# Hybrid decoder layer on one core: FFN weight loads behind the memory output's, GpSimd sums begun behind the second merged tile, last splits and tail reordered

## The chip, the cores and the metric

The kernel runs on 1 core of one Trainium2 chip. The metric is device time in microseconds (us). Engines are named as in the profile: PE is TensorE (matmuls; PEld its weight loads), DVE is VectorE, ACT is ScalarE, POOL is GpSimd, SP issues DMAs. A name with a q (SPq, POOLq) is the engine's queue that issues DMAs. Every engine works through its own list of instructions in order; semaphores tie the lists together.

## What is computed

One layer of a decoder for 512 tokens of width 1024, in float32, cut to what matters:

```python
h = rms_norm(x, g_mix)
q, k, v, u, gb, gc, ga, gB = split(h @ w_in)            # 3 x 512, 3 x 512, 2 x 1024 columns
o_a = stick_breaking_attention(q, k, v)                 # 8 heads of 64, causal
y_b = gb * causal_conv3(gc * u)                         # 512 channels
merged = sigmoid(ga) * (o_a @ w_a) + sigmoid(gB) * (y_b @ w_b)
x = x + merged @ w_mix_out
x = x + cross_attention(rms_norm(x), rms_norm(mem)) @ w_mem_o    # 4 heads of 256, 256 memory tokens
gate, up = split(rms_norm(x) @ w_ffn_in)                # 2 x 2816 columns
x = x + (silu(gate) * up) @ w_ffn_out
return rms_norm(x, g_final)
```

## The kernel before, in words

Matmuls run in a reduced float32 format, so each factor is split into a high part (a cast on ACT) and a low part (the difference, on DVE), and each product is three matmuls: high x high, high x low, low x high (`mm3`, L148 to L151). A weight tile therefore goes SP load (`wr`), ACT cast (`wh`), DVE subtraction (`wl`), PE; `load_w` (L133 to L146) does this for all weights up to the memory output, and the pool behind `wr`, `wh` and `wl` has 4 buffers each.

The stages, in order of time: value projection; projections of q, k, conv and gates, interleaved with the attention; the merge (L479 to L497: eight tiles m, each two gate projections, the two branch products `br`, two sigmoids, products with the gates on DVE at L493, their sum at L494, and a split `mh`, `ml`); key projection of the memory (`km`, L500 to L512) and value projection (`vm`, L513 to L525); the mix output and residual; the memory's queries and attention (L587 to L651); the memory output and residual (L653); the FFN (L657 to L893); the output product (`run`, L898); and the tail with the last norm (L1038 to L1071).

FFN input and output products are computed with seven products of half tiles in place of eight. For the output product this needs sums of blocks of `w_ffn_out`. GpSimd makes them ahead (L450 to L461): for each of 11 pieces j it loads 1 MB into a tile `pre`, adds four times in place (L458) and stores the tile to a DRAM tile `sums` (L460). The pool `prepool` has two such tiles. It opens when the attention's pool `lpool` closes (L450) and when it closes `fpool` takes its memory (L462).

`ffn_load` (L664) loads one FFN tile m on SP in three loads: `ws` (L670), `wg` (L672), `a` (L674; `a22` in the code); a DMA of GpSimd (L675) adds onto `ws`. Tiles of m = 0 and 1 are loaded for the first eight products. Most of them take `wr` buffers, and some, the `a` of m = 0, the `ws` of m = 1 and the `wg` of m = 2, take tiles of `fpool`.

Outside the two stretches under `manual_schedule` (the first tiles, and all from L848 on) a scheduler sets the order of each engine's list; `after` (L101) adds an ordering without a semaphore. From L848 on PE, ACT and DVE follow the order in which the code is written. There, `uses` (L760) lists the products (m, i) of FFN tile m; `reads` and `second` take a product's bank into SBUF, `evict` applies the norm, Silu and the product with the other half, in three parts. `first_parts` (L831) is a list of preparations for the output product: `out_pair` loads and splits two blocks of weights, `act_first` and `act_second` split activations. The first of them are popped among the last FFN products (L883), the others beside `run`.

In the output product, `run(i, j)` is product i of seven on piece j (six matmuls). After products 0 to 3, the loop from L1002 runs products 4, 6 and 5, with `act_third`, `out_pair` and `out_one` as their preparations, and adds two transposed tiles of the residual per step (`turned`, `begin`). The tail adds product 5, forms the squares on ACT, the factor of the last norm from them (`rstd`: a sum on DVE, Ln and Exp on ACT, a correction step on DVE), scales the eight output tiles and stores them.

Of the kernel before, what the change touches and what calls it, by code (L numbers as in the profile page):

```python
# [33 lines left out]
FIRST = 4  # L34

# [4 lines left out]
def hybrid_layer(ctx: ExitStack, tc: tile.TileContext, xT_d, memT_d, cols_d, wv_d, win_d,  # L40
# [58 lines left out]
    exps, casts, lead, lows = [], [], [], []  # L99
# [33 lines left out]
    def load_w(src, cols=P):  # L133
# [3 lines left out]
        i = nc.sync.dma_start(raw, src)  # L137
        if count[1] < FIRST:
            count[1] += 1
            chained(i)  # L140
# [312 lines left out]
    with tc.tile_pool(name="prepool", bufs=2) as prepool:  # L453
        for j in range(NJ):
            t = prepool.tile([P, 4, 512], F32, tag="pre", name=nm("pre"))
            nc.gpsimd.dma_start(t, wfo_d[j])
# [5 lines left out]
    fpool = ctx.enter_context(tc.tile_pool(name="fpool", bufs=2))  # L462

    mg = []
# [15 lines left out]
    for m in range(KD):  # L480
# [14 lines left out]
        merged.append(split(sig[0], "m"))  # L495
        if m % 2 == 1:
            mem_split(m // 2)  # L497

# [165 lines left out]
    def ffn_load(m):  # L664
# [5 lines left out]
        nc.sync.dma_start(s13, a[:, 2:3, :].broadcast_to([P, 2, 512]))  # L670
        wg = wg[0].tile([P, 2, 512], F32, tag=wg[1], name=nm("wg"))
        nc.sync.dma_start(wg, a[:, 0:2, :])  # L672
        a22 = fpool.tile([P, 512], F32, tag="w2", name=nm("a22"), bufs=4)
        nc.sync.dma_start(a22, a[:, 3, :])  # L674
# [173 lines left out]
    with tc.manual_schedule(engines={mybir.EngineType.PE, mybir.EngineType.Activation,  # L848
# [6 lines left out]
        for n, (m, i) in enumerate(uses):  # L855
# [6 lines left out]
            elif i == 5 and m == NF - 1:  # L862
                reads(m, i)
                second(m)
            else:
                if i == 1 and m > 0:
                    second(m - 1)
                reads(m, i)
# [14 lines left out]
            if n >= len(uses) - 6 and n % 2 == len(uses) % 2:  # L883
                first_parts.pop(0)()
            if (m, i) == (NF - 2, 6):
                evict(m, 0)
                evict(m, 1)
            if (m, i) == (NF - 1, 5):
                evict(NF - 2, 2)
        evict(NF - 1, 0)  # L890
# [79 lines left out]

        def turned(t, h):
# [6 lines left out]
        def begin(t, h, x):  # L978
            if t < 2 and h == 0:
# [3 lines left out]
                nc.gpsimd.tensor_tensor(out=l1[t], in0=l1[t], in1=gain[0], op=ALU.mult)  # L983
# [17 lines left out]
        lag = 1  # L1001
        for j in range(NJ):  # L1002
            if j + 2 < NJ and j > 0:
                act_third(j + 1)
            if j < NJ - 2:
                run(4, j)
                if j == 0:
                    uv = [plus("uv", res[2][s2], u[s2]) for s2 in range(2)]
                    res[5] = [ztile("p5") for _ in range(2)]
                settle()  # L1010
                if j > 0:
                    out_pair(j + 1, sums[j + 1][:, 2:4, :], 4, 6)
                run(6, j)
                out_one(j + 1)
                if j >= lag:
# [119 lines left out]
```

## Time and profile before

| What | Value |
|---|---|
| Median of 3 runs | 896.61 us (893.87 to 896.71) |
| The profiled execution's own time | 894.85 us |
| Its span on the core | 893.1 us |
| TensorE busy | 853.7 us (96%) |
| VectorE busy | 647.2 us (72%) |
| ScalarE busy | 459.2 us (51%) |
| GpSimd busy | 145.4 us (16%) |
| Granted TensorE clock, mean | 0.98 |
| DMA, mean | 156 GB/s |

The profile is of one execution; its span is the time from its first to its last instruction on the core, and 1.75 us of its own time lie around that. Start times in the rows are us from the span's start. A row of waits gives the waiting engine and line, what ended the wait, the total in us, how often, and the longest. A row of the timeline gives start, duration, engine, line and operation, output and inputs, and in brackets how long the engine sat idle before it and what ended that. A busy TensorE isn't one at full speed: its clock is shown apart, as granted by the throttle.

### The profile page before, as it was taken

Reading aid. Unit: us, or ns where it says so; the run is one execution under the profiler, and the core shown is the slowest. Engines: PE = TensorE matmul, PEld = TensorE weight load, DVE = VectorE, ACT = ScalarE, POOL = GpSimd, SP = SyncE. Lnnn points to the kernel's source line nnn. Section 1 sums busy time; section 2 is a strip of 40 time slices with the busy share of each in tenths; the row PEclk is TensorE's granted clock in tenths of the full one; section 3 lists DMA queues with packets and bytes.
Section 4 is the critical chain, followed back from the end, with each engine's and each line's share of the span. In section 5 each row is a group of like instructions: output and inputs, shape, how many; then the busy total and the mean of one; then the engine's idle time right before and its main releaser. Section 6 shows DMA issues by size and latency. Waiting matters only on the chain.

```text
span 893.1 us, 12825 instructions
## 1 busy us (share of the span) xinstructions
PE 853.7 (96%) x4840; PEld 743.2 (83%) x4840; DVE 647.2 (72%) x1080; ACT 459.2 (51%) x842; POOL 145.4 (16%) x179
## 2 busy tenths in 40 slices
PE   9999999998999964999999999999999999999994
PEld 7888888886888854888888889999999999888883
DVE  7778879988655634645554678977888788799765
ACT  7466666664233223444344466555554555566544
POOL 0022211216566550000000010111111110000011
PEclk9999999999999996999999999999999999999998
DMA  7322222227787648542212153777766773366532
GB/s 284 122 103 83 83 83 64 78 72 283 276 300 283 236 189 282 182 149 95 95 48 71 48 129 83 189 198 178 181 179 178 191 189 94 116 216 209 189 130 95
DMA packets 48574, 139.54 MB, mean 156 GB/s; under 512 B 4608, under 2 KB 6656, under 8 KB 45696
## 3 DMA queue, kind: packets, MB, share of 16 engines
q1 hardware_dynamic: 38576, 103.04, 34.4%
q0 software_dynamic: 9216, 34.61, 14.7%
q10 hardware_dynamic: 720, 1.07, 0.3%
q8 instruction: 38, 0.62, 0.3%
q14 instruction: 24, 0.20, 0.1%
HBM read 125.07 MB, written 13.63 MB: 155 GB/s over the span
## 4 chain that ended last, share of the span: by engine, by line
PE 80%; POOL 8%; DMA 7%; DVE 2%; ACT 1%; issue 1%; SPq 0%; ACTq 0%; DVEq 0%; POOLq 0%
PE z L706 14%; PE p L903 11%; POOL pre L458 8%; PE y L706 7%; DMA pre<-in_w_ffn_out_dram 6%; PE pr L150 5%; PE pr L149 5%; PE pr L151 5%; PE v L706 4%; PE r L150 3%; PE r L149 3%; PE r L151 3%; PE v L255 3%; PE mq L149 2%; PE mq L150 2%; PE mq L151 2%
## 5 line engine op out<-in xcount | busy, mean ns | idle before, releaser
L144 ACT CAST wh<-wr 128x1024 fp32r<-128x1024 f32 x84 | 88.0, 1051 | 188.7 <-issue 77.8
L145 DVE TENSOR_TENSOR wl<-wr,wh 128x1024 fp32r<-128x1024 f32 x84 | 108.6, 1295 | 59.9 <-ACT wh L144 59.8
L149 PE MATMUL pr<-xgh,wh 128*128 128x512 f32 x288 | 113.3, 393 | 2.3 <-DVE g L493 2.3
L150 PE MATMUL pr<-xgl,wh 128*128 128x512 f32 x288 | 113.2, 393 | 0.0
L151 PE MATMUL pr<-xgh,wl 128*128 128x512 f32 x288 | 112.7, 391 | 0.0
L675 POOL DMA_DIRECT2D ws<-in_w_ffn_in_dram x22 | 26.5, 1207 | 358.9 <-DVE c L535 170.4
L458 POOL TENSOR_TENSOR pre<-pre 128x512 f32<-128x512 f32 x44 | 67.4, 1536 | 28.4 <-DMA pre<-in_w_ffn_out_dram 26.1
L706 PE MATMUL z<-xdh,wf 128*128 128x256 f32 x352 | 70.5, 283 | 0.2 <-ACT sb L727 0.2
L149 PEld LDWEIGHTS pr<-xgh,wh 128*128 128x128 f32 x288 | 54.4, 189 | 13.9 <-DVE g L493 2.7
L151 PEld LDWEIGHTS pr<-xgh,wl 128*128 128x128 f32 x288 | 54.5, 189 | 11.5
L150 PEld LDWEIGHTS pr<-xgl,wh 128*128 128x128 f32 x288 | 54.5, 189 | 10.9
L706 PEld LDWEIGHTS z<-xdh,wf 128*128 128x128 f32 x352 | 58.0, 192 | 0.5 <-ACT sb L727 0.4
L727 ACT COPY sa<-z 128x256 f32<-128x256 f32 x44 | 16.4, 372 | 79.3 <-PE z L706 78.4
L706 PE MATMUL z<-xdl,wf 128*128 128x256 f32 x176 | 49.8, 283 | 0.0
L696 DVE TENSOR_TENSOR wf<-s,wf 128x512 fp32r<-128x512 f32 x44 | 30.3, 691 | 25.8 <-ACT wf L695 25.7
L813 DVE TENSOR_TENSOR wl<-wr,wh 128x1024 fp32r<-128x1024 f32 x33 | 40.7, 1232 | 9.8 <-ACT wh L812 9.8
L812 ACT CAST wh<-wr 128x1024 fp32r<-128x1024 f32 x33 | 34.6, 1049 | 11.3 <-PE p L903 5.5
L149 PE MATMUL km<-mgh,wh 128*128 128x256 f32 x64 | 19.2, 304 | 19.3 <-DVE km L506 19.3
L706 PE MATMUL y<-xoh,wf 128*128 128x256 f32 x176 | 35.6, 285 | 1.8 <-DVE sb L737 1.8
L706 PE MATMUL z<-xch,wf 128*128 128x256 f32 x176 | 35.4, 284 | 0.1
L706 PE MATMUL y<-xch,wf 128*128 128x256 f32 x176 | 35.4, 283 | 0.0
L706 PE MATMUL v<-xoh,wf 128*128 128x256 f32 x176 | 35.4, 283 | 0.0
(315 smaller groups left out, 2437.0 us busy)
## 6 DMA issues: line engine op xcount, KB each, us to landing
wr<-in_w_in_dram SPq DMA_DIRECT2D x36, 512.0 KB, 3.5
pre<-in_w_ffn_out_dram POOLq DMA_DIRECT2D x11, 1024.0 KB, 8.4
sums<-pre POOLq DMA_DIRECT2D x11, 1024.0 KB, 4.9
ws<-in_w_ffn_in_dram SPq DMA_DIRECT2D x22, 512.0 KB, 3.7
wg<-in_w_ffn_in_dram SPq DMA_DIRECT2D x22, 512.0 KB, 4.1
ws<-in_w_ffn_in_dram POOLq DMA_DIRECT2D x22, 512.0 KB, 5.9
wr<-sums SPq DMA_DIRECT2D x22, 512.0 KB, 4.6
wr<-in_w_ffn_out_dram SPq DMA_DIRECT2D x16, 512.0 KB, 3.7
```

The source lines that it names most:

```text
L144: after(nc.scalar.copy(h2, raw), lead[-1:])
L145: lows.append(nc.vector.tensor_tensor(out=l2, in0=raw, in1=f(h2), op=ALU.subtract))
L149: nc.tensor.matmul(ps, a[0], b[0], start=start, stop=False, **kw)
L150: nc.tensor.matmul(ps, a[0], b[1], start=False, stop=False, **kw)
L151: nc.tensor.matmul(ps, a[1], b[0], start=False, stop=stop, **kw)
L255: nc.tensor.matmul(vps[t], xg[k][a][:, sl], wv[k][b], start=k == 0 and (a, b) == (0, 0), stop=k == KD - 1 and a == 1)
L458: nc.gpsimd.tensor_tensor(out=t[:, a, :], in0=t[:, a, :], in1=t[:, b, :], op=ALU.add)
L696: nc.vector.tensor_tensor(out=w[:, 1, :], in0=raw, in1=f(w[:, 0, :]), op=ALU.subtract)
L706: nc.tensor.matmul(ps[:, :HS], a, b, start=i < 3 and k == 0 and j == 0, stop=k == KP - 1 and j == 2, skip_group_check=True)
L812: nc.scalar.copy(hi, raw)
L813: nc.vector.tensor_tensor(out=lo, in0=raw, in1=f(hi), op=ALU.subtract)
L903: nc.tensor.matmul(res[i][s2], a[:, ts], b, start=j == 0 and n == 0, stop=j == NJ - 1 and n == 2)
```

## The change

Four things are changed.

- `load_w` keeps its load instructions in a list. The first FFN loads (m < 2) are ordered behind the sixth from last of them, `loads[-6]`, which is the third of the eight loads of the memory output.
- The sums are made by a function that is called in the merge, behind the split of the second merged tile (`SUMS_AT = 1`). For the first two pieces a copy of one column of that tile into `pre` on GpSimd makes the load wait for it. `prepool` opens as before, and closes, with `fpool` opening, behind the merge.
- Among the last FFN products, `second` of the last tile is called one product earlier and ahead of the eviction, and the first parts are popped after products -6, -3 and -1 from the end, not -6, -4 and -2.
- In the output product the third split and the pair of weights are prepared for j + 2 in every step, not for j + 1. In the tail, the factor of token tiles 2 and 3 is begun before the last product, its correction step comes later (`rstd_end`), the second product for tiles 2 and 3 gets its gain on GpSimd (`gained`), scalings are divided anew between ACT and DVE (`how`), and all stores but one go through SP.

```diff
+SUMS_AT = 1
...
         i = nc.sync.dma_start(raw, src)
+        loads.append(i)
...
+    def weight_sums(prepool):
         for j in range(NJ):
             t = prepool.tile([P, 4, 512], F32, tag="pre", name=nm("pre"))
+            if j < 2:
+                nc.gpsimd.tensor_copy(t[:, 0, 0:1], f(merged[SUMS_AT][0])[:, 0:1])
             nc.gpsimd.dma_start(t, wfo_d[j])
...
         merged.append(split(sig[0], "m"))
+        if m == SUMS_AT:
+            weight_sums(prepool)
...
-        nc.sync.dma_start(s13, a[:, 2:3, :].broadcast_to([P, 2, 512]))
+        i = nc.sync.dma_start(s13, a[:, 2:3, :].broadcast_to([P, 2, 512]))
+        if m < 2:
+            after(i, [loads[-6]])
...
-            elif i == 5 and m == NF - 1:
-                reads(m, i)
-                second(m)
...
-            if n >= len(uses) - 6 and n % 2 == len(uses) % 2:
-                first_parts.pop(0)()
             if (m, i) == (NF - 2, 6):
+                second(NF - 1)
                 evict(m, 0)
                 evict(m, 1)
             if (m, i) == (NF - 1, 5):
                 evict(NF - 2, 2)
+            if n - len(uses) in (-6, -3, -1):
+                first_parts.pop(0)()
...
+        for j in range(NJ - 2):
+            run(4, j)
...
+            settle()
+            act_third(j + 2)
+            run(6, j)
+            out_pair(j + 2, sums[j + 2][:, 2:4, :], 4, 6)
+            if j > 0:
+                run(5, j - 1)
+            out_one(j + 1)
...
+        for s2 in range(2):
+            onto(ys[2 + s2, 0], res[6][s2], 2 + s2, ys[2 + s2, 0])
+            square(2 + s2, 0)
+            gained(2 + s2, 0)
...
+        rstd(hi)
+        end(0)
+        rstd_end(hi)
+        store(2, 1, "act")
+        store(2, 0, "dve")
+        rstd(t0)
+        end(1)
+        store(3, 1, "act")
+        rstd_end(t0)
+        store(0, 1, "both")
+        store(0, 0, "act")
+        rstd(t1)
+        store(3, 0, "dve")
+        rstd_end(t1)
+        store(1, 1, "both")
+        store(1, 0, "act")
```

The same treatment as `s13` gets goes for `wg` and `a22`. How the lists of instructions change is shown at three places.

SP in the key projection, before: `wr` from `w_mem_k` are key weights, `a`, `ws` and `wg` FFN loads.

```order
L137 DMA wr_3246<-in_w_mem_k_dram 128x1024
L674 DMA a_4971<-in_w_ffn_in_dram 128x512
L670 DMA ws_4976<-in_w_ffn_in_dram 128x2x512
L137 DMA wr_3281<-in_w_mem_k_dram 128x1024
L672 DMA wg_5090<-in_w_ffn_in_dram 128x1024
L137 DMA wr_3318<-in_w_mem_k_dram 128x1024
L137 DMA wr_3353<-in_w_mem_k_dram 128x1024
```

SP in the memory output, of the changed kernel: `wr` from `w_mem_o` are that stage's weights.

```order
L138 DMA wr_4585<-in_w_mem_o_dram 128x1024
L138 DMA wr_4620<-in_w_mem_o_dram 128x1024
L138 DMA wr_4678<-in_w_mem_o_dram 128x1024
L690 DMA a_4973<-in_w_ffn_in_dram 128x512
L682 DMA ws_4978<-in_w_ffn_in_dram 128x2x512
L686 DMA wg_5092<-in_w_ffn_in_dram 128x1024
L138 DMA wr_4715<-in_w_mem_o_dram 128x1024
```

The three FFN loads left the key projection, where now the eight key loads follow each other, and stand behind the third load of the memory output.

ACT at the end of the FFN, before: `wh` are weight casts of `out_pair`, `f01h` and `f26h` activation casts, `fg` the Silu of FFN tiles 20 and then 21.

```order
L812 CAST wh_7885<-wr_7883 128x1024
L163 CAST f01h_7889<-a_5551 128x512
L746 ACTIVATE fg_7669<-fg_7669 128x512
L812 CAST wh_7923<-wr_7921 128x1024
L163 CAST f26h_7929<-a_5285 128x512
L796 CAST f_7933<-n_7927 128x256
L746 ACTIVATE fg_7799<-fg_7799 128x512
L108 ACT_TABLE_LOAD
L812 CAST wh_7972<-wr_7970 128x1024
```

The same place on ACT in the changed kernel:

```order
L764 ACTIVATE fg_7671<-fg_7671 128x512
L830 CAST wh_7903<-wr_7901 128x1024
L165 CAST f01h_7907<-a_5553 128x512
L830 CAST wh_7943<-wr_7941 128x1024
L165 CAST f26h_7949<-a_5287 128x512
L814 CAST f_7953<-n_7947 128x256
L764 ACTIVATE fg_7801<-fg_7801 128x512
L109 ACT_TABLE_LOAD
L830 CAST wh_7974<-wr_7972 128x1024
```

The first Silu moved ahead of the casts of the second piece (`wh_7903`, `f01h_7907`); the last Silu, the table load and the cast of that piece's second pair stay where they were.

DVE in the tail, before: `u_8504` is an eviction of product 5, `var` to `rf` the factor, `elh` two scalings.

```order
L961 SCALAR_TENSOR_TENSOR u_8504<-p_8538,nrt,u_8504 128x512
L1040 TENSOR_TENSOR var_8928<-ss 128x2
L120 TENSOR_SCALAR rv_8930<-var_8928 128x2
L122 TENSOR_TENSOR ra_8932<-ry_8931 128x2
L123 SCALAR_TENSOR_TENSOR ra_8932<-ra_8932,rv_8930 128x2
L125 SCALAR_TENSOR_TENSOR rf_8933<-ra_8932,ry_8931 128x2
L1049 SCALAR_TENSOR_TENSOR elh_8564<-elh_8564,rf_8933,gain_8523 128x512
L1049 SCALAR_TENSOR_TENSOR elh_8641<-elh_8641,rf_8933,gain_8523 128x512
L961 SCALAR_TENSOR_TENSOR u_8506<-p_8539,nrt,u_8506 128x512
```

The same place of the changed kernel:

```order
L1054 TENSOR_TENSOR rms<-ss 128x2
L1057 TENSOR_SCALAR rms<-rms 128x2
L977 SCALAR_TENSOR_TENSOR u_8506<-p_8540,nrt,u_8506 128x512
L1063 TENSOR_TENSOR rms<-rms 128x2
L1064 SCALAR_TENSOR_TENSOR rms<-rms 128x2
L1066 SCALAR_TENSOR_TENSOR rms<-rms 128x2
L1074 TENSOR_SCALAR elh_8572<-elh_8572,rms 128x512
L1054 TENSOR_TENSOR rms<-ss 128x1
L1057 TENSOR_SCALAR rms<-rms 128x1
L977 SCALAR_TENSOR_TENSOR u_8508<-p_8541,nrt,u_8508 128x512
```

The factor's sum is ahead of the first eviction, and one scaling with a scalar stands ahead of the last eviction in place of two with a gain.

121 lines of the change are left out of this document (55 added, 66 removed).

## The prediction

> **What bounds the kernel now.** I read the page first (span, busy shares, slices), then what TensorE waited for, then the order of time on SP, GpSimd, ScalarE and VectorE around each wait, then windows for the granted clock.
>
> The page's span and TensorE's row of slices, then TensorE's list of waits (engine, line, releaser: us in total, times, longest):
>
> ```profile
> span 893.1 us, 12825 instructions
> PE   9999999998999964999999999999999999999994
> ...
> PE km L149 <- DVE km L506: 19.3, 1, 19.3
> PE pr L149 <- DVE g L493: 2.3, 1, 2.3
> PE y L706 <- DVE sb L737: 1.8, 1, 1.8
> ...
> PE p L903 <- DVE wl L813: 0.9, 2, 0.7
> ```
>
> TensorE is at work nearly everywhere: the time is its work plus these few waits, plus what the clock loses after them, plus an end of 12 us without matmuls. One wait is large; the page shows it as the 4 in the row of slices.
>
> Its cause stands in the order of time. SP's DMA queue, GpSimd, ScalarE, TensorE (start, us, what; in brackets the idle time before it and what ended it):
>
> ```profile
> 295.59 3.32 SPq L137 DMA_DIRECT2D wr<-in_w_mem_k_dram  x2
> 335.73 0.33 SPq L674 DMA_DIRECT2D a<-in_w_ffn_in_dram  x1
> ...
> 202.34 0.75 POOL L456 DMA_DIRECT2D pre<-in_w_ffn_out_dram  x1
> 304.00 8.29 POOL L458 TENSOR_TENSOR pre<-pre 128x512 f32<-128x512 f32 x5 [4.05 <-DMA pre<-in_w_ffn_out_dram]
> 331.37 0.57 POOL L460 DMA_DIRECT2D sums<-pre  x1 [0.30 <-POOL pre L458]
> ...
> 343.27 1.04 ACT L144 CAST wh<-wr 128x1024 fp32r<-128x1024 f32 x1 [22.13 <-DMA wr<-in_w_mem_k_dram]
> ...
> 346.30 0.58 PE L149 MATMUL km<-mgh,wh 128*128 128x256 f32 x1 [19.26 <-DVE km L506]
> ```
>
> SP issues two key-weight loads from 295.59 and then nothing until 335.73, when a first FFN load (L674) goes out. That load's tile takes the memory of the pool in which GpSimd forms its sums (202.34 to 331.37), so it waits for the last of them, and four of the eight key weights stand behind it. TensorE eats the split weights it has and stops for 19.26 us. The name L506 in the wait is not the cause: VectorE stood behind the split of a weight that hadn't come.
>
> **The change part by part.**
>
> *The first FFN loads go behind the third load of the memory output.* The order shows that the queue is free for the key weights. The row that released the loads, 335.73, is far past: in the trace before, that third load is issued at 451.13, and the sums are long done. Three issues of 0.3 to 0.4 us each now stand before the fourth load of the memory output, in a stretch where SP waits for buffers anyway; I cost them at nothing, and 1.2 us if that cover were gone. What goes is 19.26 us and the slow clock behind it:
>
> ```profile
> 451.13 0.33 SPq L137 DMA_DIRECT2D wr<-in_w_mem_o_dram  x1
> ...
> 218.80:222.60 3.80, 3.80 (x12) 2.94 (x11) 3.77 (x3) 1.38 (x3) 3.62 (x4) 0.55 0.68 281
> 768.40:772.10 3.70, 3.70 (x14) 3.11 (x13) 3.43 (x7) 1.16 (x3) 0.00 (x0) 0.54 0.22 67
> 346.30:351.80 5.50, 5.50 (x26) 5.50 (x27) 3.36 (x5) 2.95 (x5) 0.00 (x0) 0.50 1.08 302
> ```
>
> (Windows: length, busy us and count of PE, PEld, DVE, ACT, POOL, then granted clock, DMA share, GB/s.) After the stall the clock was 0.50 for 5.5 us: 5.5 x 0.50 = 2.75 us lost. Term: -22.0.
>
> *The sums begin at the second merged tile.* That tile is made from the L493 pair now at 217.57, which comes about 2 us sooner as shown below, and cast some 2 us behind it, at about 217. So GpSimd starts 15 us later than at 202.34, and its last store is at about 346 instead of 331.37. Two effects. First, VectorE is free of GpSimd while the first two merged tiles are made. VectorE now (start, us):
>
> ```profile
> 212.01 1.72 DVE L494 TENSOR_TENSOR g<-g,g 128x512 f32<-128x512 f32 x1
> 213.66 2.32 DVE L145 TENSOR_TENSOR wl<-wr,wh 128x1024 fp32r<-128x1024 f32 x1
> 217.57 1.28 DVE L493 TENSOR_TENSOR g<-br,g 128x512 f32<-128x512 f32 x2
> ...
> 361.69 1.23 DVE L145 TENSOR_TENSOR wl<-wr,wh 128x1024 fp32r<-128x1024 f32 x1 [0.58 <-ACT wh L144]
> 363.57 0.42 DVE L506 TENSOR_TENSOR km<-km,rmb 128x256 f32<-128x256 f32 x1 [0.32 <-PE km L151]
> 364.57 1.22 DVE L145 TENSOR_TENSOR wl<-wr,wh 128x1024 fp32r<-128x1024 f32 x1 [0.58 <-ACT wh L144]
> 365.71 0.42 DVE L511 TENSOR_TENSOR kml<-km,kmh 128x256 fp32r<-128x256 f32 x1
> 367.44 1.22 DVE L145 TENSOR_TENSOR wl<-wr,wh 128x1024 fp32r<-128x1024 f32 x1 [1.31 <-ACT wh L144]
> 370.16 1.22 DVE L145 TENSOR_TENSOR wl<-wr,wh 128x1024 fp32r<-128x1024 f32 x1 [1.50 <-ACT wh L144]
> ```
>
> With GpSimd adding, a split of 128x1024 takes 2.32 us, without it 1.22; an addition of half that length with both inputs in SBUF (L494) takes 1.72, where one of the same length that reads PSUM (L493, two in 1.28) takes 0.64. So an operation with both inputs in SBUF pays about 1.1 us whatever its length, and one that reads PSUM nothing. Without the three such payments ahead of L493 (L494, L145 and the split after it) the bank that TensorE waits for at L493 is free about 3 us sooner, and its gap of 2.3 us closes, with the slow clock behind it (3.80 us at 0.55: 1.71). Term: -4.0. Nothing else is late there: the next matmul needs only that bank.
>
> Second, the adds that stood beside the merge now stand beside the key projection, which moves up by the 4 us just won: two of its tiles were done where TensorE stopped at 327.0 (346.30 - 19.26), so with 2.88 us each (below) it starts at 321.3 - 4, about 317, and ends eight tiles on, at 340. The code gives the adds in groups of eight (two blocks of four); the last full group starts at 304.00 now, so at about 319 then, inside the key projection, and four more fall into the value projection. A key tile costs VectorE 1.22 + 0.42 (L145, L511) and 0.42 for the eviction (L506, which reads PSUM), 2.06 in all, against 2.88 us of matmuls (from L145 at 361.69 to the next at 364.57). With 1.1 on each of the two splits it is 4.26. Eight adds can hit eight such splits, four tiles: at most 4 x (4.26 - 2.88) = 5.5 us, at least nothing, because four split weights and two banks stand ready. Two banks forgive about 2.5 of the 5.5, and GpSimd rests between adds; the nearest row is the merge itself, where the same adds cost TensorE nothing after the first group. Term: +1.5. In the value projection a load costs VectorE 1.22 + 1.1 of its 2.72 (from 367.44 to 370.16): nothing.
>
> By the Trainium skill ("SBUF — State Buffer", Who interferes with whom) a VectorE operation with two SBUF inputs and a GpSimd operation that reads SBUF exclude each other for the whole instruction; by it each split waits a whole add, as the 1.1 us of these rows do, and the sum would take the full +5.5.
>
> *The last splits.* The wait of 1.8 us is TensorE waiting for VectorE to read a bank behind a split. Now that read (`second`) is ahead of the split, so the gap and its slow clock (3.70 us at 0.54: 1.70) go from 767. But they come back at the f26 product of the second pair (j=1). TensorE, VectorE, ScalarE, TensorE:
>
> ```profile
> 767.42 0.39 PE L706 MATMUL y<-xoh,wf 128*128 128x256 f32 x1 [1.79 <-DVE sb L737]
> ...
> 768.67 1.22 DVE L813 TENSOR_TENSOR wl<-wr,wh 128x1024 fp32r<-128x1024 f32 x1 [1.30 <-ACT wh L812]
> 773.26 0.69 DVE L744 TENSOR_TENSOR fg<-fg,r0b 128x512 f32<-128x512 f32 x1
> 778.49 0.68 DVE L164 TENSOR_TENSOR f26l<-a,f26h 128x512 fp32r<-128x512 f32 x1
> ...
> 773.98 0.63 ACT L746 ACTIVATE fg<-fg 128x512 f32<-128x512 f32 x1 [3.31 <-DVE fg L744]
> 774.63 1.28 ACT L108 ACT_TABLE_LOAD   x1
> 775.93 1.05 ACT L812 CAST wh<-wr 128x1024 fp32r<-128x1024 f32 x1
> ...
> 779.23 0.50 PE L903 MATMUL p<-wh,f26l 128*128 128x512 f32 x1
> ```
>
> The product of f26 for j=1 needs the weight cast at 775.93 and f26l, ready at 778.49 + 0.68; TensorE takes it at 779.23, without slack. That cast stands behind the table load, the load behind the last Silu (773.98), the Silu behind the last L744 on VectorE (773.26). In the new order ScalarE does the Silu of tile 20 before the first split of j=1. The gap at 767.42 began at 765.63, so the product before ended at about 764.2 (1.44 us, half of a key tile's 2.88, for 12 matmuls). Two evictions and L744 follow on VectorE (0.35 + 0.35 + 0.69: 765.6), the Silu (0.63: 766.25) and the cast (1.05: 767.3) on ScalarE, and VectorE's split can start at 767.3. From there to the last L744 stands what now takes from 768.67 to 773.26 (4.6 us), and the split of j=1 with its f01l (1.22 + 0.68, overlapping to 1.75): L744 at about 773.6, 0.3 later than before. TensorE is there 3.5 us sooner, at about 775.5, waits until about 779.5, and the clock drops behind that as behind 1.79 us; part of the slow stretch falls into the wait. Net 0.3 + about 1.3. Term: +1.6; if the chain were early enough, -(1.8 + 1.7) = -3.5.
>
> *The tail.* The third split and the pair of each j come one step ahead of need, so the 0.9 us at L813 goes. Then TensorE, VectorE, ScalarE at the end:
>
> ```profile
> 880.68 0.39 PE L903 MATMUL p<-wq,f45l 128*128 128x512 f32 x1
> 881.62 1.42 DVE L1049 SCALAR_TENSOR_TENSOR elh<-elh,rf,gain 128x512 f32<-128x512 f32 x2
> 882.95 0.74 DVE L961 SCALAR_TENSOR_TENSOR u<-p,nrt,u 128x512 f32<-128x512 f32 x1
> ...
> 886.70 0.72 ACT L1047 ACTIVATE l<-l,rf 128x512 f32<-128x512 f32 x1 [0.61 <-DVE rf L125]
> 889.00 0.72 ACT L1047 ACTIVATE uv<-uv,rf 128x512 f32<-128x512 f32 x1 [0.42 <-ACT l L1047]
> 889.75 0.34 ACTq L1051 DMA_DIRECT2D out_dram<-uv  x1
> ```
>
> The last eviction waits 1.8 us (881.1 to 882.95) behind two scalings; now only a short one (a row that is multiplied by its gain on GpSimd already) is ahead, and ends before. From eviction to the last store's issue were 6.8 us, with three scalings on ScalarE one behind the other after the factor; now one is left, two having moved ahead of the last factor, which they delay by about 0.5: some 5.1 us. Term: -0.9 - 1.8 - 1.7 = -4.4 (-3 to -5). The two new GpSimd products lie beside matmuls.
>
> Sum: -22.0 - 4.0 + 1.5 + 1.6 - 4.4 = -27.3. Against the profiled execution's 893.1 of span, 894.85 in all, that is 867.6. The runs shown (896.71, 893.87, 896.61) and the profiled one have a mean of 895.5, which I take: **868.2**.
>
> **The rivals.**
>
> *The last splits pay*: for it, that my margin is a quarter of a microsecond in a chain of ten steps; against, that every step of it has its row. -3.5 in place of +1.6: 863.1.
>
> *The key projection pays for the adds*: every add of the fifth group meets a split, +5.5, and one drop of the clock, 1.7, in place of 1.5: 873.9. For it the fixed 1.1 us of the rows; against it the buffers, and the adds' own gaps. By the Trainium skill's exclusive port (the page above) this would be the usual case; the merge, with the same adds, shows no wait after 219.
>
> *The stall stays although the loads have moved*, because the sums' traffic and the key weights come too late together. In the window from 346.30 302 GB/s were moved; key weights (512 KB per 2.88 us, 182 GB/s) and the sums' 4 MB left for those 31 us ask for about 320. If the whole -22.0 were lost: 890.2. Against: TensorE lived 28 us on what was loaded (SP's last issue before the hole ends at 298.9, TensorE stops 19.26 us before 346.30).
>
> *Slower*: the clock stays down through key and value projections, because waits of TensorE as long as 1.8 us recur within each 3.7 us. Both stages, 8 x 2.88 + 8 x 2.72 = 44.8 us, would take twice that: 868.2 - 1.5 + 44.8 = 911.5. It decides when VectorE costs each tile 1.8 us more than TensorE all along; the fifth group allows 1.4 in four tiles, the value projection none, and at half clock TensorE itself needs 5.76 a tile and no longer waits.
>
> **How the numbers follow.** My forecast has 0.52, the last splits paying 0.18, the key projection paying 0.22, the stall staying 0.06, slower 0.02. From 863.1 to 873.9 the first three hold 0.92; with the tail's and the first gap's spread of 2 to 3 us outside, the range is 861 to 877. A change of 0.3% (2.7 us) is about what a measurement here can tell. Faster 0.97, same 0.01, slower 0.02.
>
> **What would show it.** Right: SP's key loads without a hole; no wait of TensorE over 2 us from 300 to 350; none at the first gate projection behind the second merged tile; no wait at the last `y`, but one of 3 to 4 us at the second pair's f26, with a clock of about 0.5 behind it; last store about 5 us behind the last matmul. Wrong: a wait for L506 or L145 of over 3 us in the key projection; a hole in SP's issues before the memory output's fourth load; the second pair's cast before 775 on the old scale.

## The result and the profile after

The changed kernel takes **868.56 us** (median of 4 runs, 866.01 to 869.89), the kernel before it on the same chip 896.66 us (4 runs, 893.87 to 898.0): a ratio of 0.9687, with a 95% interval from 0.9655 to 0.9719. Predicted were 868.2 us. Two later comparisons of the same pair gave 868.86 against 893.7 us (0.9713, from 0.9691 to 0.9735) and 867.65 against 893.41 us (0.9706, from 0.9679 to 0.9733).

The profiled execution took 869.89 us with a span of 868.2, where before it was 894.85 and 893.1: 24.9 us less of span, and my sum for it said 27.3. So the mechanisms have to be looked at one by one. First the page of the changed kernel: span, TensorE's slices with their granted clock, and its list of waits (us in total, times, longest).

```profile
span 868.2 us, 12834 instructions
...
PE   9999999999999999999999999999999999899995
...
PEclk9999999999999999999999999999999999899998
...
PE km L151 <- DVE km L518: 2.6, 4, 0.8
PE p L919 <- ACT f26h L165: 1.4, 1, 1.4
...
PE p L919 <- DVE a L772: 0.7, 1, 0.7
PE br L151 <- DVE g L500: 0.5, 1, 0.5
```

The 4 in the row of slices is gone, with its wait of 19.3 us. The waits of 2.3 us at `pr` and of 1.8 us at `y` are gone too. In their place stand four short ones in the key projection and two at `p`; these two lie in the only slice but the last in which the clock is an 8.

SP's queue in the key projection, the key weights and the value weights behind them, and where the first FFN loads went:

```profile
289.81 26.58 SPq L138 DMA_DIRECT2D wr<-in_w_mem_k_dram  x6
...
321.31 21.47 SPq L138 DMA_DIRECT2D wr<-in_w_mem_v_dram  x8
...
413.10 14.99 SPq L138 DMA_DIRECT2D wr<-in_w_mem_o_dram  x3
428.40 0.33 SPq L690 DMA_DIRECT2D a<-in_w_ffn_in_dram  x1
...
433.19 12.44 SPq L138 DMA_DIRECT2D wr<-in_w_mem_o_dram  x2
```

The hole from 299 to 335.73 is closed. Three FFN loads go out from 428.40 on, between the third and the fourth load of the memory output, and TensorE has no wait there: the cost that I put at nothing is nothing.

For the rest I read where TensorE's stages begin: the start of the first matmul of each stage in the timeline of both kernels, and the differences.

| Stage | before | after | change | predicted |
|---|---|---|---|---|
| up to the first `km` matmul | 317.99 | 313.21 | -4.8 | -4.0 |
| key projection, to the first `vm` matmul | 45.38 | 26.78 | -18.6 | -22.0 + 1.5 |
| from there to the first FFN product | 180.52 | 180.54 | 0 | 0 |
| FFN, to the first f01 matmul of the third pair | 237.74 | 239.96 | +2.2 | +1.6 |
| output product, to the last matmul | 99.05 | 97.54 | -1.5 | -0.9 |
| from the last matmul's start to the end of the span | 12.42 | 10.17 | -2.3 | -3.5 |

The sum of the changes is -25.0, with the span's 24.9. Three places need their rows.

**The key projection.** VectorE, TensorE and GpSimd in the changed kernel, and a window over the stage (length, busy us and count of PE, PEld, DVE, ACT, POOL, then clock, DMA share, GB/s):

```profile
322.97 1.97 DVE L147 TENSOR_TENSOR wl<-wr,wh 128x1024 fp32r<-128x1024 f32 x1
324.86 1.52 DVE L523 TENSOR_TENSOR kml<-km,kmh 128x256 fp32r<-128x256 f32 x1
...
326.63 1.96 DVE L147 TENSOR_TENSOR wl<-wr,wh 128x1024 fp32r<-128x1024 f32 x1
...
326.86 0.36 PE L151 MATMUL km<-mgh,wh 128*128 128x256 f32 x1 [0.62 <-DVE km L518]
...
318.90 8.61 POOL L464 TENSOR_TENSOR pre<-pre 128x512 f32<-128x512 f32 x5 [3.03 <-DMA pre<-in_w_ffn_out_dram]
...
328.06 5.35 POOL L464 TENSOR_TENSOR pre<-pre 128x512 f32<-128x512 f32 x3
...
313.20:340.00 26.80, 24.22 (x194) 23.28 (x193) 24.51 (x27) 12.06 (x18) 15.74 (x12) 1.00 0.87 316
```

From 318.90 to 333.41 GpSimd adds with one break of 0.6 us, and VectorE is busy for 14.30 of these 14.51 us: a split of 128x1024 takes 1.97 where it took 1.22, a split of 128x256 1.52 where it took 0.42, and a tile 3.66 us (326.63 - 322.97) where TensorE needs 2.88. TensorE waits for the eviction at L518 in four tiles. The clock is 1.00 all the same.

**The second pair's f26.** ScalarE, then TensorE, and a window over what follows:

```profile
750.81 0.63 ACT L764 ACTIVATE fg<-fg 128x512 f32<-128x512 f32 x1 [1.73 <-DVE fg L762]
751.46 1.28 ACT L109 ACT_TABLE_LOAD   x1
752.76 1.04 ACT L830 CAST wh<-wr 128x1024 fp32r<-128x1024 f32 x1
...
751.96 0.50 PE L919 MATMUL p<-wh,f 128*128 128x512 f32 x1 [0.72 <-DVE a L772]
754.37 0.79 PE L919 MATMUL p<-wh,f26h 128*128 128x512 f32 x1 [1.44 <-ACT f26h L165]
756.05 0.80 PE L919 MATMUL p<-wh,f26l 128*128 128x512 f32 x1
...
754.40:760.40 6.00, 5.86 (x12) 4.02 (x13) 6.00 (x10) 3.57 (x6) 0.00 (x0) 0.50 0.40 130
```

The chain stands as the prediction had it: Silu, table load, cast, split, and the product with f26l at 756.05, which is 23.18 us ahead of the 779.23 of before. Behind it the clock is 0.50 for 6 us.

**The end.** VectorE and the last issues:

```profile
855.92 0.69 DVE L1054 TENSOR_TENSOR rms<-ss 128x2 f32<-128x2 f32 x1 [0.79 <-ACT sq L984]
856.64 1.22 DVE L1057 TENSOR_SCALAR rms<-rms 128x2 f32<-128x2 f32 x1
857.77 0.74 DVE L977 SCALAR_TENSOR_TENSOR u<-p,nrt,u 128x512 f32<-128x512 f32 x1
...
859.74 0.74 DVE L977 SCALAR_TENSOR_TENSOR u<-p,nrt,u 128x512 f32<-128x512 f32 x1
...
855.30 2.54 POOL L989 TENSOR_TENSOR elh<-elh,gain 128x512 f32<-128x512 f32 x2
...
858.03 0.39 PE L919 MATMUL p<-wq,f45l 128*128 128x512 f32 x1
...
864.25 0.39 ACTq L1079 DMA_DIRECT2D out_dram<-l  x1
...
864.28 0.33 SPq L1079 DMA_DIRECT2D out_dram<-u  x1
```

From the last eviction to the last issue it is 4.54 us where it was 6.80. But the last eviction still starts 1.71 us behind the last matmul (2.27 before): two operations on two columns took 0.69 and 1.22 us beside GpSimd's two products by the gain, and each ended with one of these products (856.61 and 857.86, the products at 856.59 and 857.84).

### The profile page after: what moved, and what is told of

The parts are those of the page before. It is cut to its first block, busy times and chain, and to the rows that moved or that the text cites. A ratio compares the mean times of both kernels' runs of the same rounds, so it can differ in the third digit from the quotient of the medians.

```text
span 868.2 us, 12834 instructions
## 1 busy us (share of the span) xinstructions
PE 850.9 (98%) x4840; PEld 739.7 (85%) x4840; DVE 659.8 (76%) x1080; ACT 460.5 (53%) x842; POOL 153.1 (18%) x183
## 4 chain that ended last, share of the span: by engine, by line
PE 92%; DVE 4%; issue 2%; ACT 1%; DMA 1%; SPq 0%; POOL 0%; DVEq 0%; ACTq 0%; POOLq 0%
PE z L724 14%; PE p L919 10%; PE pr L151 8%; PE pr L152 8%; PE pr L153 8%; PE y L724 7%; PE v L724 4%; PE r L152 3%; PE r L151 3%; PE r L153 3%; PE v L257 2%; PE br L151 2%; PE mq L153 2%; PE mq L151 2%; PE mq L152 2%
## 5 line engine op out<-in xcount | busy, mean ns | idle before, releaser
L147 DVE TENSOR_TENSOR wl<-wr,wh 128x1024 fp32r<-128x1024 f32 x84 | 116.2, 1387 | 34.5 <-ACT wh L146 34.3
L464 POOL TENSOR_TENSOR pre<-pre 128x512 f32<-128x512 f32 x44 | 71.5, 1629 | 29.2 <-DMA pre<-in_w_ffn_out_dram 26.9
L745 ACT COPY sa<-z 128x256 f32<-128x256 f32 x44 | 16.4, 373 | 78.9 <-PE z L724 78.0
L714 DVE TENSOR_TENSOR wf<-s,wf 128x512 fp32r<-128x512 f32 x44 | 30.3, 691 | 25.7 <-ACT wf L713 25.6
L831 DVE TENSOR_TENSOR wl<-wr,wh 128x1024 fp32r<-128x1024 f32 x33 | 40.4, 1223 | 7.4 <-ACT wh L830 7.4
L724 PE MATMUL z<-xf,wf 128*128 128x256 f32 x264 | 35.4, 283 | 0.0
```

Source lines behind the costliest of these rows:

```text
L147: lows.append(nc.vector.tensor_tensor(out=l2, in0=raw, in1=f(h2), op=ALU.subtract))
L464: nc.gpsimd.tensor_tensor(out=t[:, a, :], in0=t[:, a, :], in1=t[:, b, :], op=ALU.add)
L714: nc.vector.tensor_tensor(out=w[:, 1, :], in0=raw, in1=f(w[:, 0, :]), op=ALU.subtract)
L724: nc.tensor.matmul(ps[:, :HS], a, b, start=i < 3 and k == 0 and j == 0, stop=k == KP - 1 and j == 2, skip_group_check=True)
L831: nc.vector.tensor_tensor(out=lo, in0=raw, in1=f(hi), op=ALU.subtract)
```

## The experiments

All medians are in us, with the kernel before run beside them on the same chip. "FFN" is the stage from the first FFN product to the third pair's f01, "key" the key projection, "end" from the last matmul's start, all from the profile.

| Kernel | Median | Before | Ratio (95%) | key | FFN | end |
|---|---|---|---|---|---|---|
| loads only | 872.06 | 893.25 | 0.9757 (0.9737 to 0.9777) | 23.29 | 237.76 | 12.45 |
| sums only | 901.72 | 893.25 | 1.0091 (1.0071 to 1.0111) | 57.69 | 237.75 | 12.50 |
| old last splits | 865.97 | 893.25 | 0.9691 (0.967 to 0.9711) | 25.22 | 237.74 | 10.11 |
| old tail | 871.49 | 893.25 | 0.975 (0.9727 to 0.9773) | 26.28 | 239.09 | 12.47 |
| as changed, again | 868.86 | 893.7 | 0.9713 (0.9691 to 0.9735) | 26.30 | 239.20 | 10.13 |
| late sums | 865.62 | 893.7 | 0.9678 (0.9656 to 0.97) | 23.30 | 239.51 | 10.13 |
| early chain | 862.37 | 893.7 | 0.9641 (0.9619 to 0.9663) | 26.10 | 233.94 | 10.17 |
| gain on VectorE | 867.16 | 893.7 | 0.9694 (0.9671 to 0.9717) | 25.73 | 239.08 | 8.95 |
| all of these | 858.39 | 893.46 | 0.9609 (0.9591 to 0.9627) | 23.29 | 233.94 | 9.11 |
| table later | 864.76 | 893.46 | 0.9679 (0.966 to 0.9698) | 26.35 | 238.02 | 10.09 |
| table later, again | 864.8 | 893.41 | 0.9671 (0.9645 to 0.9696) | 25.23 | 236.46 | 10.14 |
| as changed, third | 867.65 | 893.41 | 0.9706 (0.9679 to 0.9733) | 25.24 | 239.42 | 10.1 |

### The load order alone

The kernel before with the list of loads, and the three loads of `ffn_load` ordered behind its sixth from last:

```diff
+        loads.append(i)
...
-        nc.sync.dma_start(wg, a[:, 0:2, :])
+        i = nc.sync.dma_start(wg, a[:, 0:2, :])
+        if m < 2:
+            after(i, [loads[-6]])
```

> The kernel before, with nothing changed but the order: the first two tiles' FFN weight loads go behind the third load of the memory output. The sums start and end as before. My theory: the 19.3 us of TensorE in the key projection and the 2.75 us of slow clock behind them go, -22.0; the gap of 2.3 us at the second merged tile, the wait at the last y and the old end stay; the last four adds of GpSimd (one block) fall into the key projection and cost two tiles 0.8 us each at most, +1.6. So 20.4 to 22 us less than the kernel before, 873.5 to 876 us. Rival, the stall is traffic that comes too late: a wait of over 10 us stays in the key projection, and the time is above 885.

Measured: 872.06 us, 21.2 less than the kernel before on the same chip, inside the 20.4 to 22 that I expected (the median lies just under my 873.5 to 876 us, as the kernel before has 893.25 here). TensorE's largest wait, and SP's queue in this kernel:

```profile
PE pr L150 <- DVE g L494: 1.9, 1, 1.9
...
294.62 25.58 SPq L137 DMA_DIRECT2D wr<-in_w_mem_k_dram  x6
```

No wait in the key projection; it takes 23.29 us where it took 45.38, -22.1, so my term of -22.0 stands by itself. The last block's adds cost TensorE nothing here (I had allowed 1.6): the splits of two tiles were slowed, and the buffers covered that. That the stall was traffic is out.

### The sums alone

The call of `weight_sums` behind the second merged tile, with its copies and `fpool` behind the merge, as in the diff of the change; the FFN loads as before.

> The kernel before, with the sums of GpSimd started behind the second merged tile and nothing else: the FFN loads stay where they were on SP's queue. My theory: the last sum is stored some 15 us later (about 346 to 351 where it was 331), SP's queue is shut that much longer (first FFN load at about 350 where it was 335.73), and TensorE starts again in the key projection at about 361 where it was 346.3. What is won at the second merged tile (about 4.8 us) is lost in the same stall, which grows to about 19.3 + 14.8 + 4.8 = 39 us. So 15 us slower than the kernel before, about 911. Rival, the sums do not hold SP's queue: the stall stays as it is and the gap at the merge goes, some 4.8 us faster, about 891.

Measured: 901.72 us, 8.5 slower. TensorE's wait, and SP's queue:

```profile
PE km L150 <- DVE km L516: 32.5, 1, 32.5
...
289.82 21.72 SPq L138 DMA_DIRECT2D wr<-in_w_mem_k_dram  x5
352.10 0.33 SPq L684 DMA_DIRECT2D a<-in_w_ffn_in_dram  x1
...
353.02 0.39 SPq L138 DMA_DIRECT2D wr<-in_w_mem_k_dram  x1
```

The sign and the mechanism are mine: the first FFN load goes out at 352.10, 16.4 us later than before, and the stall grows by 13 us. The size is not: I took SP's order for unchanged, and it isn't. Seven of the eight key weights now stand ahead of the FFN load (two issued before the five of the first row), where four did, so TensorE gets further before it stops and has only 7.5 us of the stage left when it starts again at 363.37. Outside `manual_schedule` the list of SP is the scheduler's, and moving the sums moved the FFN loads in it. So the two edits are no sum of parts: the earlier merge (-4.8) shows only once the queue is free.

### The last splits as before

The changed kernel with the old pops, ahead of the evictions, and with the last tile's `second` behind product 5:

```diff
-                second(NF - 1)
                 evict(m, 0)
...
-            if n - len(uses) in (-6, -3, -1):
+            if n >= len(uses) - 6 and n % 2 == len(uses) % 2:
                 first_parts.pop(0)()
```

> The changed kernel with the last splits of the FFN in their old order (all else as changed). My theory: the new order cost 2.2 us more than it gained, so this is about 2 us faster than the changed kernel, about 866.3: the wait of 1.8 us at the last y is back, with about 1.7 us of slow clock, and the two waits (0.72 and 1.44 us) ahead of the second pair's f26 with their slow clock of 6 us are gone. Rival, the last splits pay and the waits behind them have another cause (the sums or the load order): the wait at y comes back and those at f26 stay, some 3.5 us slower, about 872.

Measured: 865.97 us. The FFN stage is 237.74 us, 1.3 to 2.2 less than in the six profiles of the table and of the result that have the changed order (239.08 to 239.96). The old wait is back, and the two of 0.72 and 1.44 us ahead of f26 are gone. The row of the wait, and a window behind it:

```profile
742.31 0.39 PE L724 MATMUL y<-xoh,wf 128*128 128x256 f32 x1 [1.79 <-DVE sb L755]
...
742.30:746.00 3.70, 3.69 (x22) 3.32 (x23) 2.44 (x5) 2.15 (x4) 0.00 (x0) 1.00 0.21 74
```

The slow clock that I expected behind this wait did not come: it is 1.00, here and in the two kernels above, where the profile of before has 0.54 for 3.7 us. TensorE waits 0.25, 0.25 and 0.43 us at the second pair's f26 instead, and the stage is as long as before (237.74). So the chain to f26l sets the end of the stage, and the slow clock behind the last `y` cost nothing in it.

So the new last splits cost, as I said, and the rival that they pay is out. The medians alone (865.97 here, 867.65 to 868.86 for the change in other comparisons) would not settle 2 us; the stage does.

### The tail as before

The output product's loop from product 4 on, and all behind it, as in the kernel before.

> The changed kernel with the output products' loop and the tail of the kernel before (all else as changed). My theory: from the last matmul to the end it takes back 3.8 us, so about 872.3: last store some 6.8 us behind the last eviction instead of 4.5, an eviction 1.8 us late, and 0.9 us of waits at L831's splits. Rival, the shorter tail is only the splits that come one step earlier: 0.9 us, about 869.4.

Measured: 871.49 us. From the third pair's f01 to the last matmul 99.02 us (97.54 with the change), from there to the end 12.47 (10.17): 3.8 us in all, as expected, of which 1.5 are the splits that come a step earlier and 2.3 the end.

### The changed kernel again

> The changed kernel once more, beside the three that follow. Its key projection took 26.8 us from its first matmul to the first of the value projection (25.2 and 26.3 in two variants with the same key projection, 23.3 where most adds were over). My theory, that the adds hit VectorE's splits by chance of phase: again 25 to 27 us, and the rest of the program as in the first profile. If the spread came from the variants' edits: 26.8 again.

Measured: 868.86 us, key projection 26.30, FFN 239.20. With a third profile (below, 25.24) and the variants whose key projection is the same, this stage takes 25.2 to 26.8 us for the same instructions; in the shortest the group of adds began at 321.02, in the longest at 318.90. In all nine profiles with this key projection it takes 25.2 to 25.7 us where the adds begin 7.5 to 8.3 us behind the first `km` matmul, and 26.1 to 26.8 where they begin 5.0 to 6.0 behind it. So the time goes with where the adds fall, as I held, though no run moves that place by itself.

### The sums of the last blocks behind the key projection

The second call stands behind the loop of the key projection; the last argument is the tile that the copies wait for.

```diff
-            weight_sums(prepool)
+            weight_sums(prepool, range(8), merged[m][0])
...
+    weight_sums(prepool, range(8, NJ), km[-1][0])
+    prestack.close()
```

> The changed kernel with the sums of the last three of eleven blocks held back until the last tile of the key projection is cast. They then lie beside the value projection and the residual behind it. My theory: the waits for L518 in the key projection go (23.3 us from its start to the value projection's where it was 26.8), the value projection has room for them (VectorE 1.22 + 1.1 of 2.72 us a load), so 1.5 to 3.5 us faster than the changed kernel. Rival, the adds cost the same wherever they lie beside splits: no change, the waits turn up in the value projection or the residual.

Measured: 865.62 us, 3.2 less than the changed kernel beside it. Windows over the key projection and the value projection, with the columns as above:

```profile
313.10:336.40 23.30, 23.30 (x193) 23.07 (x192) 17.55 (x27) 12.04 (x18) 0.58 (x1) 1.00 0.67 218
336.40:358.20 21.80, 21.80 (x98) 18.05 (x97) 12.99 (x12) 10.47 (x12) 15.33 (x13) 1.00 0.83 307
```

TensorE is busy for all of 23.30 and 21.80 us, and its list has no wait in the residual behind. GpSimd adds for 15.33 us beside the value projection and that costs nothing, because VectorE has time to spare there (12.99 of 21.80 us busy, where in the changed kernel's key projection it was 24.51 of 26.80). So the price in the key projection is that of the adds, and all of its 1.9 to 3.5 us could be avoided.

### The FFN's last chain made earlier

`tables`, the table load, goes behind the first two pairs of the output product.

```diff
                 second(NF - 1)
                 evict(m, 0)
+                first_parts.pop(0)()
                 evict(m, 1)
...
+            if (m, i) == (NF - 1, 6):
+                evict(m, 0)
-            if n - len(uses) in (-6, -3, -1):
+            if n - len(uses) in (-6, -1):
                 first_parts.pop(0)()
-        evict(NF - 1, 0)
         evict(NF - 1, 1)
-        tables = log_exp_tables(silus[-1])
```

> The changed kernel with the chain of the FFN's last tile made earlier: the second pair's first split ahead of tile 20's Silu, the last tile's product with the factor ahead of the first pair's second split, and the table load behind the output products' second pair. My theory, that this chain (Silu, table load, cast, split) sets the waits ahead of the second pair's f26: both waits (0.72 and 1.44 us) and the slow clock behind them go, from the second form product of the FFN to the third pair's f01 it takes about 234.5 to 236 us where it took 240.0, so 4 to 5.5 us faster than the changed kernel. Rival, the wait is on VectorE's total work there, whatever the order: under 1.5 us faster, with waits of as much at f26l.

Measured: 862.37 us, 6.5 less than the changed kernel beside it. A window from the first `p` matmul to the third pair's f01, then ScalarE:

```profile
742.20:753.10 10.90, 10.90 (x50) 9.05 (x49) 10.83 (x20) 6.32 (x11) 0.00 (x0) 1.00 0.44 144
...
746.64 0.63 ACT L764 ACTIVATE fg<-fg 128x512 f32<-128x512 f32 x1
...
756.65 1.28 ACT L109 ACT_TABLE_LOAD   x1
```

TensorE never waits there, at full clock: 10.90 us where the changed kernel took 16.92 (743.57 to 760.49). VectorE is busy for 10.83 of them, so there is no room left; but its total was not the limit, the order was. The FFN stage, 233.94 us, is a little below the 234.5 to 236 that I expected, 5.3 us shorter than in the profile beside it (the rest of the difference between the two profiles lies in stages that this edit leaves as they were), and shorter than before the change by 3.8: the 3.5 us that the last splits were to pay were there to be had.

### The gain on VectorE

`store(3, 0)` is changed as `store(2, 0)` is.

```diff
             square(2 + s2, 0)
-            gained(2 + s2, 0)
...
-        store(2, 0, "dve")
+        store(2, 0, "both")
```

> The changed kernel without GpSimd's two products by the gain at the end (2.54 us at 855.30); VectorE multiplies by the gain in the two scalings instead (0.74 us where 0.49). My theory, that GpSimd's products slow VectorE's tiny operations in the factor (0.69 and 1.22 us where 0.15 and 0.17) and so the last evictions: these take 0.2 us again, the eviction that starts at 857.77 starts about 1 us sooner, and the end is 0.5 to 1 us sooner. Rival, the tiny operations are not on the path: no change, or 0.3 us later by the longer scalings.

Measured: 867.16 us, with an end of 8.95 us, 1.2 less, a little more than the 0.5 to 1 that I expected. The same VectorE operations as above in this kernel:

```profile
853.24 0.16 DVE L1053 TENSOR_TENSOR rms<-ss 128x2 f32<-128x2 f32 x1 [0.79 <-ACT sq L984]
853.43 0.17 DVE L1056 TENSOR_SCALAR rms<-rms 128x2 f32<-128x2 f32 x1
...
855.91 0.74 DVE L977 SCALAR_TENSOR_TENSOR u<-p,nrt,u 128x512 f32<-128x512 f32 x1
```

The tiny operations take 0.16 and 0.17 us again, and the last eviction starts 0.56 us behind the last matmul (855.35), 1.15 sooner. The longer scalings cost nothing visible.

### All of these

The three edits above and one more: `store(2, 0)` behind the last eviction.

> All that helped in one: the late sums, the earlier chain of the FFN's last tile, the gain multiplied on VectorE, and the scaling of one tile moved behind the last eviction. If the parts add up: -3.2 - 5.3 - 1.2 - 0.4 = -10.1 against the changed kernel, about 858.8. Rival, the parts share a slack (a stage that comes sooner waits for a weight that doesn't): less than 8 us faster, above 861, with a new wait of TensorE in the FFN or in the output products.

Measured: 858.39 us, against an expected 858.8. The parts add up, and this is the fastest version: 35.1 us below the kernel before. The one edit that was not tried alone shows no gain (an end of 9.11 against 8.95).

### The table load alone

The added line stands behind the first two pairs of the output product.

```diff
         evict(NF - 1, 1)
-        tables = log_exp_tables(silus[-1])
...
+        tables = log_exp_tables(silus[-1])
```

> The changed kernel with one step alone moved out of the chain of the FFN's last tile: the table load (1.28 us) stands behind the output products' second pair; the order of the casts and splits is the changed kernel's. My theory: the cast for the second pair comes 1.28 us sooner, the wait of 1.44 us ahead of f26 shrinks to 0.2 to 0.5, the wait of 0.72 us stays, and gaps as short as that left the clock alone elsewhere (0.91 and 0.69 us), so the slow clock goes too: 3.5 to 4.5 us faster than the changed kernel, about 865. Rival, the clock drops already on the 0.72 us so shortly after the last rows of the FFN, or on both together: some 1.3 us faster, with a granted clock near 0.55 behind.

Measured: 864.76 us, but an FFN stage of 238.02 in the profile, only 1.2 to 1.9 less than with the change. The waits shrank as I expected, to 0.68, 0.24 and 0.43 us, and the clock dropped nevertheless (two of TensorE's rows, and a window behind):

```profile
750.69 0.50 PE L918 MATMUL p<-wh,f 128*128 128x512 f32 x1 [0.68 <-DVE a L772]
...
753.37 0.80 PE L918 MATMUL p<-wh,f26l 128*128 128x512 f32 x1 [0.43 <-DVE f26l L166]
...
753.40:756.60 3.20, 3.20 (x8) 2.52 (x9) 3.20 (x5) 2.68 (x4) 0.00 (x0) 0.50 0.46 161
```

The profiled execution was also the slowest of its five (866.44; the others 864.19 to 865.27), so it was run again, beside the changed kernel.

> The kernel with the later table load once more. Its first profile had a slow clock behind waits of 0.7, 0.24 and 0.43 us (238.0 us from the first FFN product to the third pair's f01, 1.4 us less than the changed kernel), but its median lay 4 us below the changed kernel's. If the clock drops each time: 1 to 2 us faster than the changed kernel beside it, 238.0 again. If it drops only in some executions: 3 to 4.5 us faster by the median, and the stage at 235 to 236.5 in this profile.

> The changed kernel, to stand beside the kernel with the later table load on the same chip: about 868.7 as before, 239.1 to 240 us from the first FFN product to the third pair's f01.

Measured: 864.8 us beside 867.65, and a profile with the same three waits and no drop:

```profile
750.46 0.50 PE L918 MATMUL p<-wh,f 128*128 128x512 f32 x1 [0.68 <-DVE a L772]
752.20 0.50 PE L918 MATMUL p<-wl,f26h 128*128 128x512 f32 x1 [0.25 <-DVE wl L831]
753.14 0.50 PE L918 MATMUL p<-wh,f26l 128*128 128x512 f32 x1 [0.43 <-DVE f26l L166]
...
753.10:756.60 3.50, 3.46 (x15) 2.87 (x16) 3.50 (x5) 2.76 (x4) 0.00 (x0) 1.00 0.48 153
```

The same waits, to 0.01 us, are followed by a clock of 0.50 in one execution and of 1.00 in another. The stage takes 236.46 us, inside what I had for "only in some executions"; the medians' difference, 2.85 us, lies just under the 3 to 4.5 that I had for it. So my theory holds in this execution and the rival in the other; that the clock dropped in only some of the unprofiled runs is not shown by rows. The mean granted clock of each execution points that way: 0.995 in the profiled one with the drop, 0.997 in the one without, 0.996 or 0.997 in the eight others, and 0.993 to 0.995 in all of the changed kernel.

## Why the prediction was right, step by step

The forecast case came true in the main: faster, with the stall gone and the last splits costing. The price in the key projection, 1.9 to 3.5 us, lies between the forecast's 1.5 and the rival's 5.5. The point itself, 868.2, is closer to the median than the terms deserve, and that is luck. They sum to -27.3, and the two profiled executions differ by 25.0; the median of the runs fell by 28.1 beside this kernel's first runs and by 24.8 and 25.8 in the other two pairs. Between the two profiles four terms are off by 0.6 to 2 us each. The base made up for it: I took 895.5 us for the kernel before, which has medians of 893.25 to 893.7 in the four later comparisons; from 893.5 the same sum gives 866.2, some 2 us too little.

Of the signs that I had named, the closed hole, the short waits in the key projection, and the waits gone at the merge and at the last `y` came. The wait at the second pair's f26 came as 0.72 and 1.44 us, not as one of 3 to 4, and the last store is issued 6.25 us behind the last matmul (864.28 against 858.03), not about 5.

- **The load order, -22.0.** Right: -22.1 alone (the first experiment). The rival that the stall stays is out.
- **The first gap, -4.0.** Right in kind, a little more in size: -4.8. The next `pr` product starts at once at 215.29, and the wait at `br` just ahead, 0.9 us before, is 0.5 now, which I had not counted. The kernel with the load order alone, whose merge is the old one, begins its key projection at 317.02; against it the gain is 3.8, so up to 1 us of the 4.8 may be spread between executions.
- **The adds beside the key projection, +1.5.** The term that was most wrong: 3.5 in the first profile, 3.0 and 1.9 in the others (26.78, 26.30, 25.24 against 23.3 with the adds behind the stage). "Two banks forgive about 2.5 of the 5.5, and GpSimd rests between adds" is the step that failed: GpSimd rested 0.6 us in 14.5, and TensorE waited in four tiles. The bound was fair: a tile pays 0.78 us, not 1.38, since the longer split pays 0.75 and not 1.1. I had also put the start of the key projection 3 us too late (two tiles before the stop, where the first `km` matmul of before at 317.99 makes it three); it cost nothing, as the group of adds fell inside it anyway. The Trainium skill ("SBUF — State Buffer", Who interferes with whom) says that a VectorE instruction with two SBUF inputs contends with a GpSimd instruction that reads SBUF, and one with at most one SBUF input, outside its 2-port modes, doesn't. By it the eviction L518, which reads PSUM, pays nothing (0.41 here), and both splits pay, as they do; but they pay 0.75 and 1.10 us and not the whole add of 1.3 us or more that I drew from it, and the full +5.5 did not come.
- **The last splits, +1.6.** Right: +2.2 in this profile and +1.3 to +1.8 in the other five; the experiment that undoes them gives that back. The chain of ten steps put f26l's product 0.3 us later than before on a common scale; it came 0.2 later (23.18 us sooner, where the first FFN product came 23.36 sooner). The wait fell into two parts (0.72 and 1.44 us) where I had one of 3.5 to 4, and the clock behind them was at 0.50 for 6 us and not for 3.7: from f26l's product to the third pair's f01 it took 4.44 us where it took 2.40, and that is the rest. One step of the working failed without harm: the 1.70 us of slow clock behind the wait at the last `y` were no loss. With the old order the stage took 237.74 us in the profile with that slow clock and 237.74 to 237.76 in the three without it, since the chain to f26l ends it either way.
- **The tail, -4.4.** -3.8. That "now only a short one ... is ahead, and ends before" failed: the last eviction started 0.6 us sooner and not 1.8, because GpSimd's two products, which I put "beside matmuls", also lie beside the operations on two columns, and these stretched from 0.33 to 1.91 us. The price of contention that I had used in the key projection was not applied in the tail. From eviction to last issue I had 5.1 and it was 4.54; the splits one step earlier gave 1.5 and not 0.9; from the last issue to the end it is 0.6 longer (3.92 against 3.35). Two stores are issued together there; that this is why is not shown.
- **The slower case** (a clock that stays down) did not come: four waits of 0.55 to 0.84 us, one in each 3.66 us, left the clock at 1.00.

What stays open: why the kernel before takes from 890.87 to 898.61 us. Part of the spread of the changed kernel goes with the phase of the adds.

## What to carry to other kernels

A load in an in-order queue that reuses another pool's memory waits for that pool's last user, and everything behind it waits too; look for the hole in the queue's row before believing the name in the wait, and free the queue before moving the work that shuts it (the sums alone lost 8.5 us; with the queue free they brought the key projection 3.8 us forward, from 317.02 to 313.21). GpSimd's elementwise work has a price for each VectorE operation beside it whose inputs all lie in SBUF, the tiny ones included, so put it where VectorE is half idle. When a reorder takes one wait away, follow the chain from the moved step to the next product: here it moved the wait, and moving the rest of the chain gave 5.3 us more.

## What the hardware showed that I had not expected

- Whether the clock drops is not set by the waits alone. In the kernel with the later table load, 0.68, 0.25 and 0.43 us were followed by 0.50 for 3.2 us in one execution and by 1.00 in another. The wait of 1.79 us at the last `y` was followed by 0.54 for 3.7 us in the profile of before and by 1.00 in the first three experiments; four waits of 0.55 to 0.84 us in a row were followed by 1.00. Where it drops behind such a wait, the half clock lasts 3.4 us (753.3 to 756.7 with the later table load), and in the first profile of the changed kernel twice that (753.9 to 760.7). The Trainium skill ("TensorE: Matmul & The Clock Gate", Part 1: The HAM clock gate) says that the activity window runs freely and that its phase differs from run to run, and executions that differ behind the same waits fit that; its figure of an idle window of about 3.4 us ahead of the half clock does not, since the longest wait ahead of the drop is 1.44 us in the changed kernel and 0.68 in the one with the later table load.
- VectorE's operations on 128x2 take 0.16 or 0.17 us alone and up to 1.22 us beside a GpSimd product: nearly a whole one of its 1.3 us.
